# A hybrid recurrent step on one core: two chunks in one triangular matrix, and a 128-row contraction for the samples' updates

## The chip, the cores and the metric

The kernel runs on one core of a Trainium2 chip. The metric is the device time of one execution in microseconds (us). The core has TensorE (PE in the profile, with its weight loads as PEld), VectorE (DVE), ScalarE (ACT), GpSimd (POOL) and a queue engine, SyncE (SP), which here issues nearly all DMAs. Each engine works through its own instructions in order; semaphores tie them together.

## The reference

One layer of a decoder with three token mixers fed by one projection, then a gated feed-forward part. There is one prompt of 512 tokens and a batch of 8 samples of 4 tokens each. The mixers are a gated delta rule, an mLSTM and HGRN2, with 4 heads of 128 channels each. The delta rule is what the change touches most. Cut to that:

```
G = cumsum(g);  decay = exp(G[t] - G[s]) for s <= t
A = tril(beta[t] * decay * (k k^T), -1)
rhs = beta * (v - exp(G) * (k S))
u = solve (I + A) u = rhs                  # unit lower triangular
o = exp(G) * (q S) + (tril(q k^T) * decay) u
S' = exp(G[last]) * S + (k * exp(G[last] - G))^T u
```

All three mixers end a chunk with a state update of the last form, `S' = decay * S + K^T U`. For the samples that is one update for each of 8 samples and 4 heads.

## The kernel before

**Big matrix products.** The dense products (`gemm`, `step`) run as three fp32r matmuls for each 128x128 weight tile and half of the tokens: high part by high part, high by low, low by high. Each has 272 moving columns. In the trace they are `mm_..` tiles, written 128x272. There are 165 such products, and they fill TensorE from the start to the end.

**Background work.** The mixers are Python generators that `spawn` puts beside the dense products and `drive`/`stage` advance a piece at a time, so the pieces stand between the matmuls of the dense products. A counter of estimated TensorE time (`tick`) sets the spacing: after each `yield` a generator stays away for some 3.2 of it. A scheduler of the framework then fixes the order of each engine at build time. TensorE thus executes the mixers' small matmuls (fp32, tiles `bank_..`) in a fixed place among the wide ones. If the input of one is not there, all of TensorE waits.

**The delta rule of a prompt head** (`gdn`, u = 0 to 3) works on four chunks of 128 tokens. The inverse of each unit triangular matrix is made by doubling. `small_inverse` first inverts the 16x16 blocks on the diagonal: it sends the matrix out to DRAM and back with blocks as rows, does 15 pairs of small operations on VectorE, and goes out and back again. Then POOL spreads the blocks over a block-diagonal 128x128 matrix, in both orientations X and Y, four chunks wide (`gen_g__2779` and `gen_g__2782` for head 0). Three levels of doubling follow, for blocks of 16, 32 and 64. A level is, for each of four chunks:

```
pp[c] = Nn[c]^T Y[c];  Pn = mask(pp)
z[c]  = X[c]^T Pn[c];  Y += z
z[c]  = Pn[c]^T X[c];  X += z        # not at the last level
```

Nn is the triangular matrix with its axes exchanged by a TensorE transpose (`to_tok`). That makes 12, 12 and 8 fp32 matmuls of 128x128 and 4 transposes a head. Then a chain over the chunks uses Y[c] to get u (`zb`) and the next state.

**The samples' updates** (`state_update`, once for each of 8 samples in `mlstm`, `gdn` and `hgrn`, u = 4). `stack` splits K and U into high and low parts, sends them to DRAM (`ku`), rearranges them (`k`) and loads them into the tile `kuv`. There 48 rows hold data (three products of parts, 4 heads, 4 tokens), and rows 32 to 63 were zeroed at the start, so rows 48 to 63 stay zero. `uexp` on POOL spreads U over the four heads with a mask; one fp32r matmul, contracting over the 64 rows of `kuv`, gives the update of all four heads (64x512 in the trace). For the mLSTM a second, tiny one with `nm` (64x4) updates the normaliser. A group `32x128` ahead of it (`inter`) multiplies the queries into the state, in four column groups of 32.

**Other lines that the steps touch.** `masks` loads the 0/1 masks `cu` in stretches of 512 columns through the two `y` buffers and casts them on POOL. Line 118 is the matmul helper, line 123 the transpose, line 92 the two-input elementwise helper, lines 697 to 704 the DMAs of `stack`.

Of the kernel before, what the change touches and what calls it, by code (L numbers as in the profile page):

```python
# [9 lines left out]
F32 = mybir.dt.float32  # L10
F32R = mybir.dt.float32r
# [33 lines left out]
K_BM = 640  # L45
K_HM, K_NM = K_BM, K_BM + 4
K_SG = K_BM + 8
K_BD = K_SG + 1
N_CF = K_BD + 128

U_X1, U_Y1, U_HL = 0, 128, 256
U_LV = U_HL + 7 * 64
N_CU = U_LV + 4 * 128


class Build:
# [348 lines left out]
    def gate_rows(self, ps, sign, bi, ea, rst, RB, R1, R2, rp):  # L405
        self.lab = "_ga_"
        self.act(self.identr, self.ident)
        self.act(self.nm, self.cf[:64, K_NM:K_NM + H])
# [4 lines left out]
        Z, SP, GF, T, i2, l2, m = (row() for _ in range(7))  # L413
# [18 lines left out]
        I3, i2, l2, m = (t[G3] for t in (T, i2, l2, m))  # L432
# [53 lines left out]
        c = self.cst  # L486
# [4 lines left out]
        for k, R in ((1, R2), (0, R1)):  # L491
            self.lab = "_ga_"
            b = self.bank()
# [3 lines left out]
            b = self.bank()  # L497
# [332 lines left out]

    def small_inverse(self, Nt, out):

        lab = self.lab
        z = self.dr.tile([8 * 8208], F32, tag="nt", name="nt")
        self.qs.dma_start(out=z[0:65536].rearrange("(p x) -> p x", p=128), in_=Nt.rearrange("p c t -> p (c t)"))
        yield 4
        zb = z.rearrange("(b x) -> b x", b=8)[:, 0:8192].rearrange("b (j c t) -> b j c t", j=16, c=4)
        DT = self.gen()[:32]
        D = DT[:, 0:256].rearrange("p (j i) -> p j i", j=16)
        for c in range(4):  # L840
            self.qs.dma_start(out=D[8 * c:8 * c + 8], in_=zb[:, :, c, 0:16])
# [23 lines left out]
        mk = self.cf[:, K_BD:K_BD + 128].rearrange("p (b j) -> p b j", b=8).unsqueeze(1).to_broadcast([128, 4, 8, 16])  # L865
        for x in range(2):
            t = self.slots(4)
            z = Z[:, 4 * x:4 * x + 4, :].unsqueeze(2).to_broadcast([128, 4, 8, 16])
            self.mul(t.rearrange("p c (b j) -> p c b j", b=8), z, mk, self.g)
            out.append(t)  # L870


    def gdn(self, q, k, vv, u):
        lab = "_g%d_" % u
        self.lab = lab
        prompt = u < H
        n = 4 if prompt else 1
# [48 lines left out]
        if not prompt:  # L926
            mb = lambda o: bn(self.cu[:, o:o + 128])
# [8 lines left out]
        b = self.to_tok(vv)  # L936
# [1 line left out]
        self.mul(nv, b, self.bc(nk, 128))  # L938
        yield
        if prompt:  # L940
            while len(XY) < 2:
                yield 2
            X, Y = XY
            yield self.WSP
        lv = (16, 32, 64) if prompt else (2,)
        for m in lv:
            self.lab = lab
            i = STEPS.index(m)
            pp = self.sbank(n)
            for c in range(n):  # L950
                self.mm(pp[:, c, :], Nn[:, c, :], Y[:, c, :])
            Pn = self.slots(n)
            self.mul(Pn, pp, bn(self.cu[:, U_LV + 128 * i:U_LV + 128 * i + 128]))
            yield
            self.lab = lab
            z = self.sbank(n)
            for c in range(n):
                self.mm(z[:, c, :], X[:, c, :], Pn[:, c, :])
            self.add(Y, Y, z)
            if m != lv[-1]:  # L960
                z = self.sbank(n)
                for c in range(n):
                    self.mm(z[:, c, :], Pn[:, c, :], X[:, c, :])
                self.add(X, X, z)
            yield
        self.lab = lab
        if prompt:
            S = None
# [30 lines left out]
            o = self.sbank(4)  # L999
# [4 lines left out]
        else:  # L1004
# [27 lines left out]
            o = self.sbank(1)  # L1032
# [466 lines left out]
    def run(self):  # L1499
        with self.pool("cst") as self.cst, self.pool("wp") as self.wp, self.pool("hp", 8) as self.hp, \  # L1500
# [15 lines left out]
            with self.pool("gp", self.NG1) as self.gp:  # L1516
                with self.tc.tile_pool(name="dr", bufs=2, space=bass.MemoryType.DRAM) as self.dr, self.pool("smp") as self.smp, self.pool("stp", 4) as self.stp, \
# [48 lines left out]
def _consts():  # L1566
    s = np.arange(128)[:, None]
    t = np.arange(128)[None, :]
    cf = np.zeros((128, N_CF), np.float32)
# [7 lines left out]
    def level(m):  # L1577
        return (s // (2 * m) == t // (2 * m)) & (s % (2 * m) < m) & (t % (2 * m) >= m)
# [109 lines left out]
```

## Time and profile before

| | us |
|---|---|
| median of 3 runs | 1167.66 (1166.32 to 1168.19) |
| the profiled execution | 1167.82 |
| its span, first to last instruction | 1165.8 |
| TensorE busy | 1148.9 (99%) |
| VectorE busy | 730.6 (63%) |
| ScalarE busy | 454.1 (39%) |
| GpSimd busy | 195.7 (17%) |
| mean granted TensorE clock | 0.994 of full |

How to read it: matmuls are pipelined, so what one costs the engine is the distance from its start to the start of the next one, not its own duration. A wide matmul shows 0.29 us of its own and the next starts 0.126 us later. A fp32 matmul of 128x128 has two records, so "x8" is four matmuls. The time that an instruction waits stands in brackets behind it, with what ended the wait.

### The profile page before, as it was taken

What the parts mean: (1) busy time and instruction counts of PE and PEld (TensorE: products, weight loads), DVE (VectorE), ACT (ScalarE), POOL (GpSimd) and SP (SyncE); (2) the same over time, 40 slices, a digit from 0 to 9 for tenths busy, and PEclk for the clock granted to TensorE, in tenths of its full rate; (3) what the DMA queues carried; (4) which work ended last, traced back from release to release, by engine and by line L of the source; (5) the groups of instructions that cost most, each with busy time, mean ns of one, the idle gap of its engine ahead of it and who ended that gap; (6) DMA issues with size and microseconds to landing.
All of it is one profiled execution on the core that took longest, in us unless ns stands there. A gap on an engine that the chain in (4) does not pass through costs nothing.

```text
span 1165.8 us, 23742 instructions
## 1 busy us (share of the span) xinstructions
PE 1148.9 (99%) x9249; PEld 1126.0 (97%) x9249; DVE 730.6 (63%) x1762; ACT 454.1 (39%) x890; POOL 195.7 (17%) x662
## 2 busy tenths in 40 slices
PE   8999999999999999999999999999999999999996
PEld 8999989999999999899979999999999999999996
DVE  6876588767758666687545265476765336767532
ACT  6653454525326322332323334444443224444431
POOL 3000040101010212211142001112221002222112
PEclk9999999999999999999989999999999999999998
DMA  7232343221322334411544253222222232222332
GB/s 240 73 97 84 111 124 119 70 78 55 80 81 76 116 101 140 132 55 58 144 120 131 82 169 92 89 77 88 91 92 82 76 101 88 91 91 80 91 98 77
DMA packets 51956, 114.84 MB, mean 99 GB/s; under 512 B 11557, under 2 KB 19493, under 8 KB 51749
## 3 DMA queue, kind: packets, MB, share of 16 engines
q1 hardware_dynamic: 51124, 112.41, 31.4%
q8 instruction: 73, 1.20, 0.4%
q10 hardware_dynamic: 720, 0.92, 0.2%
q14 instruction: 39, 0.31, 0.1%
HBM read 100.92 MB, written 13.57 MB: 98 GB/s over the span
## 4 chain that ended last, share of the span: by engine, by line
PE 94%; DMA 3%; issue 1%; DVE 1%; POOL 1%; SPq 0%; ACT 0%; POOLq 0%; DVEq 0%; ACTq 0%
DMA k<-ku 1%; DMA kuv<-k 1%; PE mm_fl__14120 L118 1%; PE mm_ff__11778 L118 1%; PE mm_ff__11610 L118 1%; PE mm_ff__11442 L118 1%; PE mm_ff__13664 L118 1%; PE mm_ff__14016 L118 1%; PE mm_ff__13840 L118 1%; PE mm_ff__13576 L118 1%; PE mm_ff__11274 L118 1%; PE mm_ff__13928 L118 1%; PE mm_ff__13752 L118 1%; PE mm_ff__11358 L118 1%; PE mm_ff__11862 L118 1%
## 5 line engine op out<-in xcount | busy, mean ns | idle before, releaser
L113 ACT ACTIVATE whi<-raw 128x512 fp32r<-128x512 f32 x320 | 199.6, 625 | 495.7 <-DMA raw<-in_wdn 10.2
L92 DVE TENSOR_TENSOR wlo<-raw,whi 128x512 fp32r<-128x512 f32 x320 | 220.6, 690 | 178.4 <-ACT whi L113 169.6
L110 DVE SCALAR_TENSOR_TENSOR y<-U,cols,y 128x560 f32<-128x560 f32 (+1 forms) x124 | 100.9, 815 | 21.2 <-ACT y L113 19.5
L113 ACT ACTIVATE y<-U,cols 128x560 f32<-128x560 f32 (+1 forms) x56 | 46.8, 838 | 23.5 <-DVE U L92 23.0
L1361 POOL COPY fso<-U 128x2 f32<-128x2 f32 x44 | 28.9, 656 | 79.3 <-DVE U L92 79.3
L1358 POOL COPY U<-fst 128x16 f32<-128x16 f32 x44 | 27.0, 617 | 81.3 <-DVE y L110 40.7
L113 ACT ACTIVATE sg<-y 128x560 f32<-128x560 f32 (+1 forms) x34 | 22.9, 674 | 18.6 <-DVE y L110 18.5
L110 DVE SCALAR_TENSOR_TENSOR col<-col,col 128x4 f32<-128x4 f32 (+2 forms) x146 | 24.4, 168 | 7.6 <-ACT junk L113 4.6
L113 ACT ACT_TABLE_LOAD x16 | 20.5, 1283 | 2.7 <-DVE gen_de__2292 L110 0.9
L92 DVE TENSOR_TENSOR col<-col 128x4 f32<-128x4 f32 (+2 forms) x73 | 12.8, 175 | 1.5
L92 POOL TENSOR_TENSOR tot<-tot 128x32 f32<-128x32 f32 (+5 forms) x25 | 8.2, 329 | 13.2 <-DVE gen_ph__5506 L92 9.5
L107 DVE TENSOR_SCALAR col<-col 128x4 int32<-128x4 int32 (+4 forms) x32 | 5.6, 175 | 5.3 <-ACT junk L113 4.8
L135 POOL MEMSET gen_ff__12370<- 1x1 f32 x1 | 0.1, 88 | 51.9 <-PE mm_ff__11862 L118 51.9
L1362 POOL COPY fso<-U 128x16 f32<-128x16 f32 x44 | 8.5, 194 | 0.0
L135 POOL MEMSET gen_bh__8978<- 1x1 f32 x1 | 0.1, 89 | 46.6 <-DVE gen_bh__8730 L92 46.6
L110 DVE SCALAR_TENSOR_TENSOR hlo<-xn,cols,hhi 128x544 fp32r<-128x544 f32 x8 | 6.3, 785 | 1.8 <-ACT hhi L113 1.8
L113 ACT ACTIVATE hhi<-xn,cols 128x544 fp32r<-128x544 f32 x8 | 6.0, 751 | 1.5 <-DVE xn L92 1.5
L607 POOL COPY gso<-U 128x3 f32<-128x3 f32 x12 | 3.2, 266 | 20.3 <-ACT U L113 20.3
L105 DVE TENSOR_SCALAR col<-col 128x4 int32<-128x4 int32 (+4 forms) x38 | 6.2, 162 | 0.6
L604 POOL COPY U<-gst 128x24 f32<-128x24 f32 x12 | 3.8, 318 | 14.8 <-DVE gen_g__2447 L92 5.0
L110 DVE SCALAR_TENSOR_TENSOR xin<-xin,rp,gen_nr__469 128x544 f32<-128x544 f32 x8 | 5.6, 780 | 0.0
L92 DVE TENSOR_TENSOR hlo<-xin,hhi 128x544 fp32r<-128x544 f32 x8 | 5.2, 717 | 0.0
(5021 smaller groups left out, 4804.4 us busy)
## 6 DMA issues: line engine op xcount, KB each, us to landing
raw<-in_wp SPq DMA_DIRECT2D x47, 512.0 KB, 3.8
raw<-in_wup SPq DMA_DIRECT2D x44, 512.0 KB, 3.5
raw<-in_wgt SPq DMA_DIRECT2D x24, 512.0 KB, 3.4
raw<-in_wdn SPq DMA_DIRECT2D x16, 512.0 KB, 4.0
raw<-in_wbr SPq DMA_DIRECT2D x24, 256.0 KB, 2.7
raw<-in_wout SPq DMA_DIRECT2D x8, 512.0 KB, 3.4
raw<-in_wdn SPq DMA_DIRECT2D x16, 192.0 KB, 2.4
xin<-in_xt SPq DMA_DIRECT2D x8, 272.0 KB, 6.6
```

Source lines behind the costliest of these rows:

```text
L92: (eng or self.v).tensor_tensor(out=out, in0=a, in1=b, op=op)
L105: (eng or self.v).tensor_scalar(out=out, in0=a, scalar1=s1, scalar2=None, op0=op0)
L107: (eng or self.v).tensor_scalar(out=out, in0=a, scalar1=s1, scalar2=s2, op0=op0, op1=op1)
L110: self.v.scalar_tensor_tensor(out=out, in0=a, scalar=sc, in1=b, op0=op0, op1=op1)
L113: self.s.activation(out=out, in_=a, func=func, **kw)
L118: self.pe.matmul(out, lhsT=lhsT, rhs=rhs, start=start, stop=stop)
L135: self.g.memset(x[(slice(0, 1),) * len(x.shape)], 0.0)
L604: self.g.tensor_copy(out=sv[:, :, 0:3], in_=self.gst[:, tile_i, :, :])
L607: self.g.tensor_copy(out=self.gso[:, tile_i, 0, :], in_=U[:, 512:515])
L1358: self.g.tensor_copy(out=sv[:, :, 0:2], in_=self.fst[:, i, :, :])
L1361: self.g.tensor_copy(out=self.fso[:, i, 0, :], in_=U[:, 512:514])
L1362: self.g.tensor_copy(out=self.fso[:, i, 1:9, :], in_=sv[:, :, 4:6])
```

## The change

For the prompt heads, chunks 0 and 1 share one matrix, and chunks 2 and 3 another. The even chunk's triangle lies below the diagonal (it is transposed by TensorE), the odd chunk's above it as it was; `NP` holds their sum. `small_inverse` gives one matrix W for two chunks, with the block masks now applied by VectorE from the 8-bit masks. A level of doubling is now, for each of two pairs: a transpose of W, a product of NP with the masked W, one masking operation for both (VP), one product z, one addition into W, and one masking of W for the next level. After the last level W is transposed once more, and Y of the even and odd chunks is cut out of W and of its transpose.

For the samples, `kuv`, `nm` and the mask of `uexp` have 128 rows; rows 64 to 127 are zeroed at the start, and the matmuls contract over all 128. The sample part of `gdn` computes what it did; its code is written out. The masks `cu` grow from 1216 to 1856 columns, and `cf` loses 128.

```diff
 def uexp(self, b):
-        t = self.gen(dt=F32R)[:64].rearrange("p (h e) -> p h e", h=4)
-        self.mul(t, self.ku[:, b, 128:256].unsqueeze(1).to_broadcast([64, 4, 128]),
-                 self.bc(self.cf[:64, K_HM:K_HM + 4], 128), self.g)
+        t = self.gen(dt=F32R).rearrange("p (h e) -> p h e", h=4)
+        self.mul(t, self.ku[:, b, 128:256].unsqueeze(1).to_broadcast([128, 4, 128]),
+                 self.bc(self.cf[:, K_HM:K_HM + 4], 128), self.g)
 def small_inverse(self, Nt, out):
         self.act(XY[:, 1], X.rearrange("p i j -> p j i"))
+        self.sub(X, X, self.eye, self.g)
 ...
-        mk = self.cf[:, K_BD:K_BD + 128]...to_broadcast([128, 4, 8, 16])
-        for x in range(2):
-            t = self.slots(4)
-            z = Z[:, 4 * x:4 * x + 4, :].unsqueeze(2).to_broadcast([128, 4, 8, 16])
-            self.mul(t.rearrange("p c (b j) -> p c b j", b=8), z, mk, self.g)
-            out.append(t)
+        z = Z[:, 1:4:2, :]
+        self.add(z, z, Z[:, 4:8:2, :], self.g)
+        mk = self.cu[:, U_BD:U_BD + 128]...to_broadcast([128, 2, 8, 16])
+        t = self.slots(4)
+        self.mul(t[:, 0:2, :].rearrange("p c (b j) -> p c b j", b=8), z.unsqueeze(2).to_broadcast([128, 2, 8, 16]), mk)
+        out.append(t)
 def gdn(self, q, k, vv, u):
-        bt = self.to_tok(Nt)
-        Nn = self.slots(n)
-        self.act(Nn, bt)
+        if prompt:
+            bt = self.to_tok(Nt[:, 0::2, :])
+            NP = self.slots(2)
+            self.add(NP, bt, Nt[:, 1::2, :])
 ...
-            X, Y = XY
-        for m in lv:
-            pp = self.sbank(n)
-            for c in range(n):
-                self.mm(pp[:, c, :], Nn[:, c, :], Y[:, c, :])
-            Pn = self.slots(n)
-            self.mul(Pn, pp, bn(self.cu[:, U_LV + 128 * i:U_LV + 128 * i + 128]))
-            yield
-            z = self.sbank(n)
-            for c in range(n):
-                self.mm(z[:, c, :], X[:, c, :], Pn[:, c, :])
-            self.add(Y, Y, z)
-            if m != lv[-1]:
-                z = self.sbank(n)
-                for c in range(n):
-                    self.mm(z[:, c, :], Pn[:, c, :], X[:, c, :])
-                self.add(X, X, z)
-            yield
+            W, Wm = XY[0][:, 0:2, :], XY[0][:, 2:4, :]
+            self.mul(Wm, W, mb(U_PR))
+            for i in range(len(STEPS)):
+                pp = self.sbank(4)
+                for c in range(2):
+                    self.tr(pp[:, c, :], W[:, c, :])
+                for c in range(2):
+                    self.mm(pp[:, 2 + c, :], NP[:, c, :], Wm[:, c, :])
+                VP = self.slots(4)
+                self.mul(f4(VP), f4(pp), mk.unsqueeze(2).to_broadcast([128, 2, 2, 128]))
+                yield
+                z = self.sbank(2)
+                for c in range(2):
+                    self.mm(z[:, c, :], VP[:, c, :], VP[:, 2 + c, :])
+                self.add(W, W, z)
+                if i + 1 < len(STEPS):
+                    self.mul(Wm, W, mb(U_PR + 256 * i + 256))
+                yield
+            b = self.to_tok(W)
+            Y = self.slots(4)
+            self.mul(Y[:, 0::2, :], W, mb(U_UP))
+            self.mul(Y[:, 1::2, :], b, mb(U_UP))
 def run(self):
-                    self.ku = mc.tile([64, NB, 256], F32R, name="kuv")
-                    self.nm = mc.tile([64, H], F32R, name="nm")
+                    self.ku = mc.tile([128, NB, 256], F32R, name="kuv")
+                    self.nm = mc.tile([128, H], F32R, name="nm")
                     self.g.memset(self.ku[32:64].bitcast(F32), 0.0)
+                    self.g.memset(self.ku[64:128].bitcast(F32), 0.0)
```

Two places in the order of the instructions. The first is TensorE at head 0's first level of doubling. Before, `bank_g__2980` is pp, `gen_g__2782` is Y, `gen_g__2779` X, and 3000 and 3006 belong to head 1:

```order
L118 MATMUL bank_g__2980<-gen_g__2782,gen_g__2506 128x128 x4
L118 MATMUL bank_g__3000<-gen_pg__2618,gen_pg__2746 128x128 x4
L123 MATMUL bank_g__3006<-cf,gen_pg__2618 128x128 x4
...
L118 MATMUL bank_g__3029<-gen_g__2985,gen_g__2779 128x128 x4
L118 MATMUL bank_g__3035<-gen_g__2779,gen_g__2985 128x128 x4
```

Now `gen_g__2789` holds W and masked W, `bank_g__2994` takes the transposes and the product, and `bank_g__3056` is z (3008 belongs to head 1):

```order
L125 MATMUL bank_g__2994<-cf,gen_g__2789 128x128 x2
L120 MATMUL bank_g__3008<-gen_pg__2621,gen_pg__2749 128x128
L120 MATMUL bank_g__2994<-gen_g__2789,gen_g__2508 128x128 x2
...
L120 MATMUL bank_g__3056<-gen_g__2999 128x128 x2
```

Twelve matmuls of the head became four and two transposes; the place among the wide matmuls is nearly the same. In all, `bank_g` has 238 fp32 matmuls of 128x128 before and 158 now, and 85 transposes before and 109 now.

The second place is on TensorE at the samples of HGRN2. `bank_h__7471` transposes K, which starts the way of the data through `stack`; `bank_h__7710` is the first matmul that reads `kuv`. Before, 120 wide matmuls lie between the two:

```order
L123 MATMUL bank_h__7471<-cf,smp 128x128
...
L123 MATMUL bank_h__7542<-cf,gen_h__7436 128x128 x4
L118 MATMUL bank_h__7554<-sl_h__7264,sl_h__7259 128x128
...
L118 MATMUL bank_h__7554<-gen_h__7667,xp 32x128 x4
...
L118 MATMUL bank_h__7710<-gen_h__7664,kuv 128x512
```

Now the transpose is `bank_h__7544` and the first reader of `kuv` is `bank_h__7735`:

```order
L125 MATMUL bank_h__7544<-cf,smp 128x128
...
L125 MATMUL bank_h__7560<-cf,gen_h__7488 128x128 x4
L120 MATMUL bank_h__7591<-sl_h__7305,sl_h__7300 128x128
...
L120 MATMUL bank_h__7591<-gen_h__7679,xp 32x128 x4
...
L120 MATMUL bank_h__7735<-gen_h__7676,kuv 128x512
```

There are 99 wide matmuls between them now, and seven fp32 matmuls and four transposes of heads 2 and 3 that stood between them before now stand ahead of the transpose. On the SP queue, which carries the data out and back, this stood there before:

```order
L697 DMA ku<-gen_h__7557 128x512
L698 DMA ku<-gen_h__7559 128x256
L718 DMA gen_h__7816<-in_hS 128x512
L701 DMA k_7588<-ku 4x8x3072
L718 DMA gen_h__7873<-in_hS 128x512
L718 DMA gen_h__7933<-in_hS 128x512
L163 DMA raw<-in_wgt 128x1024
L704 DMA kuv<-k_7588 16x8x256 x3
```

And now:

```order
L699 DMA ku<-gen_h__7594 128x512
L700 DMA ku<-gen_h__7596 128x256
L720 DMA gen_h__7945<-in_hS 128x512
L703 DMA k_7625<-ku 4x8x3072
L165 DMA raw<-in_wgt 128x1024
L706 DMA kuv<-k_7625 16x8x256 x2
L720 DMA gen_h__8005<-in_hS 128x512
L706 DMA kuv<-k_7625 16x8x256
```

Two loads of a sample's state that stood ahead of the loads of `kuv` are issued earlier, and one now stands ahead of the third of them.

## Rows read from the trace of the kernel before

**Rows 1.** The page, part 1: busy time and share of the span.

```profile
PE 1148.9 (99%) x9249; PEld 1126.0 (97%) x9249; DVE 730.6 (63%) x1762; ACT 454.1 (39%) x890; POOL 195.7 (17%) x662
```

**Rows 2.** Chain of waits: start us, length us, what; a dense product of 48.

```profile
635.44 6.05 PE mm_bh__8247 L118 x48
```

**Rows 3.** TensorE's timeline at a doubling: start us, us, engine line op out<-in xcount.

```profile
226.91 1.06 PE L118 MATMUL bank_g__3000<-gen_pg__2618,gen_pg__2746 128*128 128x128 f32 x8
227.80 0.60 PE L123 MATMUL bank_g__3006<-cf,gen_pg__2618 128*128 128x128 f32 x4
228.16 0.37 PE L118 MATMUL mm_bm__3318<-hhi,wlo 128*128 128x272 f32 x1
```

**Rows 4.** TensorE's timeline around two samples' updates.

```profile
456.43 0.50 PE L118 MATMUL bank_g__6079<-gen_g__5958,kuv 64*128 64x512 f32 x1
456.86 0.39 PE L118 MATMUL mm_ph__6012<-hhi,whi 128*128 128x272 f32 x1
457.08 0.29 PE L118 MATMUL mm_ph__6012<-hlo,whi 128*128 128x272 f32 x1
...
488.52 0.28 PE L118 MATMUL mm_ph__6503<-hlo,whi 128*128 128x272 f32 x1
488.74 0.50 PE L118 MATMUL bank_g__6455<-gen_g__6359,kuv 64*128 64x512 f32 x1
489.16 0.40 PE L118 MATMUL mm_ph__6503<-hhi,wlo 128*128 128x272 f32 x1
489.40 0.28 PE L118 MATMUL mm_ph__6503<-hhi,whi 128*128 128x272 f32 x1
```

**Rows 5.** TensorE's timeline: a matmul of the same width over 128 rows.

```profile
190.53 0.40 PE L118 MATMUL bank_g__2588<-rl,identr 128*128 128x512 f32 x1
190.76 0.29 PE L118 MATMUL mm_pg__2632<-hlo,whi 128*128 128x272 f32 x1
```

**Rows 6.** TensorE's timeline at HGRN2's samples; in brackets the wait ahead and its end.

```profile
567.12 0.27 PE L123 MATMUL bank_h__7471<-cf,smp 128*128 128x128 f32 x1
...
585.43 0.29 PE L118 MATMUL mm_bg__7645<-hhi,wlo 128*128 128x272 f32 x1
588.13 0.79 PE L118 MATMUL bank_h__7710<-gen_h__7664,kuv 64*128 64x512 f32 x1 [2.40 <-POOL gen_h__7664 L92]
...
589.24 0.43 PE L118 MATMUL mm_bg__7725<-gen_bg__6901,whi 128*128 128x272 f32 x1
589.47 0.43 PE L118 MATMUL mm_bg__7725<-gen_bg__6899,wlo 128*128 128x272 f32 x1
```

**Rows 7.** Windows: busy us of each engine, then granted clock, DMA share, GB/s.

```profile
580.00:600.00 20.00, 17.59 (x112) 15.87 (x112) 7.72 (x15) 3.56 (x6) 10.66 (x16) 0.83 0.47 109
```

**Rows 8.** The SP queue's timeline at the same place.

```profile
572.44 0.59 SPq L701 DMA_DIRECT2D k<-ku  x1
...
578.99 1.28 SPq L704 DMA_DIRECT2D kuv<-k  x3
```

**Rows 9.** POOL's timeline: the first spreading of U, HGRN2's, then the delta rule's.

```profile
586.93 1.15 POOL L92 TENSOR_TENSOR gen_h__7664<-kuv,cf 64x512 fp32r<-64x512 f32 x1 [12.98 <-DMA kuv<-k]
...
450.91 1.15 POOL L92 TENSOR_TENSOR gen_g__5958<-kuv,cf 64x512 fp32r<-64x512 f32 x1 [11.06 <-DMA kuv<-k]
```

**Rows 10.** TensorE's timeline: the matmul whose result the delta rule's samples send out.

```profile
435.00 0.38 PE L118 MATMUL bank_g__5816<-r,sl_g__5046 128*128 128x128 f32 x2
```

**Rows 11.** POOL's timeline: head 0's blocks are spread.

```profile
222.90 1.09 POOL L92 TENSOR_TENSOR gen_g__2779<-gen_g__2719,cf 128x512 f32<-128x512 f32 x1 [2.82 <-DMA gen_g__2719<-xy]
223.95 1.54 POOL L92 TENSOR_TENSOR gen_g__2782<-gen_g__2719,cf 128x512 f32<-128x512 f32 x1
```

**Rows 12.** VectorE's timeline: the masking of pp at two levels.

```profile
229.58 0.67 DVE L92 TENSOR_TENSOR gen_g__2985<-bank_g__2980,cu 128x512 f32<-128x512 f32 x1
...
256.22 0.69 DVE L92 TENSOR_TENSOR gen_g__3407<-bank_g__3402,cu 128x512 f32<-128x512 f32 x1 [0.87 <-PE bank_g__3402 L118]
```

**Rows 13.** Groups by line and shape: count, busy us, mean ns of one, idle before.

```profile
L92 DVE TENSOR_TENSOR gen_ph__5231<-gen_ph__5231,tot 128x256 f32<-128x256 f32 x6 | 2.6, 438 | 3.1 <-PE bank_h__5932 L118 1.1 <-PE bank_h__5870 L118 1.1 <-PE bank_h__5726 L118 0.9
```

More of the change, by code (lines that the diff above doesn't have):

```diff
@@ L32 @@
 LEVELS = (1, 2, 4, 8, 16, 32, 64)
-STEPS = (2, 16, 32, 64)
+STEPS = (16, 32, 64)
 C_LNFFN, C_LNFIN = 0, 8
@@ L47 @@
 K_SG = K_BM + 8
-K_BD = K_SG + 1
-N_CF = K_BD + 128
+N_CF = K_SG + 1
 U_X1, U_Y1, U_HL = 0, 128, 256
 U_LV = U_HL + 7 * 64
-N_CU = U_LV + 4 * 128
+U_PR = U_LV + 128
+U_UP = U_PR + 3 * 256
+U_BD = U_UP + 128
+N_CU = U_BD + 128
 class Build:
@@ L407, in gate_rows @@
         self.act(self.identr, self.ident)
-        self.act(self.nm, self.cf[:64, K_NM:K_NM + H])
+        self.act(self.nm, self.cf[:, K_NM:K_NM + H])
         G0, G1, G2, G3 = (slice(32 * i, 32 * i + 4) for i in range(4))
@@ L864, in small_inverse @@
         self.lab = lab
-        mk = self.cf[:, K_BD:K_BD + 128].rearrange("p (b j) -> p b j", b=8).unsqueeze(1).to_broadcast([128, 4, 8, 16])
-        for x in range(2):
-            t = self.slots(4)
-            z = Z[:, 4 * x:4 * x + 4, :].unsqueeze(2).to_broadcast([128, 4, 8, 16])
-            self.mul(t.rearrange("p c (b j) -> p c b j", b=8), z, mk, self.g)
-            out.append(t)
+        z = Z[:, 1:4:2, :]
+        self.add(z, z, Z[:, 4:8:2, :], self.g)
+        mk = self.cu[:, U_BD:U_BD + 128].rearrange("p (b j) -> p b j", b=8).unsqueeze(1).to_broadcast([128, 2, 8, 16])
+        t = self.slots(4)
+        self.mul(t[:, 0:2, :].rearrange("p c (b j) -> p c b j", b=8), z.unsqueeze(2).to_broadcast([128, 2, 8, 16]), mk)
+        out.append(t)
     def gdn(self, q, k, vv, u):
@@ L922, in gdn @@
         self.lab = lab
-        bt = self.to_tok(Nt)
-        Nn = self.slots(n)
-        self.act(Nn, bt)
-        if not prompt:
-            mb = lambda o: bn(self.cu[:, o:o + 128])
+        mb = lambda o: self.cu[:, o:o + 128].unsqueeze(1).to_broadcast([128, n // 2 or 1, 128])
+        if prompt:
+            bt = self.to_tok(Nt[:, 0::2, :])
+            NP = self.slots(2)
+            self.add(NP, bt, Nt[:, 1::2, :])
+        else:
+            bt = self.to_tok(Nt)
+            Nn = self.slots(n)
+            self.act(Nn, bt)
             self.v.copy_predicated(Y, mb(U_Y1), Nt)
@@ L940, in gdn @@
         if prompt:
-            while len(XY) < 2:
+            while not XY:
                 yield 2
-            X, Y = XY
+            W, Wm = XY[0][:, 0:2, :], XY[0][:, 2:4, :]
             yield self.WSP
-        lv = (16, 32, 64) if prompt else (2,)
-        for m in lv:
             self.lab = lab
-            i = STEPS.index(m)
-            pp = self.sbank(n)
-            for c in range(n):
-                self.mm(pp[:, c, :], Nn[:, c, :], Y[:, c, :])
-            Pn = self.slots(n)
-            self.mul(Pn, pp, bn(self.cu[:, U_LV + 128 * i:U_LV + 128 * i + 128]))
+            self.mul(Wm, W, mb(U_PR))
@@ new lines, in gdn @@
+            for i in range(len(STEPS)):
[5 more added lines that the diff above has]
+                VP = self.slots(4)
+                mk = self.cu[:, U_PR + 256 * i:U_PR + 256 * i + 256].rearrange("p (k t) -> p k t", k=2)
+                f4 = lambda t: t.rearrange("p (k c) t -> p k c t", k=2)
+                self.mul(f4(VP), f4(pp), mk.unsqueeze(2).to_broadcast([128, 2, 2, 128]))
+                yield
+                self.lab = lab
+                z = self.sbank(2)
[5 more added lines that the diff above has]
+                yield
+                self.lab = lab
@@ L954, in gdn @@
+            b = self.to_tok(W)
+            Y = self.slots(4)
+            self.mul(Y[:, 0::2, :], W, mb(U_UP))
+            self.mul(Y[:, 1::2, :], b, mb(U_UP))
+        else:
+            self.lab = lab
+            pp = self.sbank(1)
+            self.mm(pp[:, 0, :], Nn[:, 0, :], Y[:, 0, :])
+            Pn = self.slots(1)
+            self.mul(Pn, pp, mb(U_LV))
             yield
             self.lab = lab
-            z = self.sbank(n)
-            for c in range(n):
-                self.mm(z[:, c, :], X[:, c, :], Pn[:, c, :])
+            z = self.sbank(1)
+            self.mm(z[:, 0, :], X[:, 0, :], Pn[:, 0, :])
@@ L959, in gdn @@
             self.add(Y, Y, z)
-            if m != lv[-1]:
-                z = self.sbank(n)
-                for c in range(n):
-                    self.mm(z[:, c, :], Pn[:, c, :], X[:, c, :])
-                self.add(X, X, z)
-            yield
+        yield
         self.lab = lab
@@ L1582, in _consts @@
     cf[:, K_NM:K_NM + H] = hm & (s // 16 != 1)
-    cf[:, K_BD:K_BD + 128] = s // 16 == t // 16
     cf[:, K_SG] = 1.0
@@ L1588, in _consts @@
     cu[:, U_Y1:U_Y1 + 128] = level(1)
+    cu[:, U_LV:U_LV + 128] = level(2)
     for i, m in enumerate(STEPS):
-        cu[:, U_LV + 128 * i:U_LV + 128 * (i + 1)] = level(m)
+        second = (s % (2 * m)) >= m
+        cu[:, U_PR + 256 * i:U_PR + 256 * i + 128] = (s // m == t // m) & np.where(second, s <= t, s >= t)
+        cu[:, U_PR + 256 * i + 128:U_PR + 256 * i + 256] = level(m) | level(m).T
+    cu[:, U_UP:U_UP + 128] = s <= t
+    cu[:, U_BD:U_BD + 128] = s // 16 == t // 16
     cu[:, U_X1:U_X1 + 128] = level(1).T
```

## The prediction

> **What bounds the kernel now.** I read the busy shares first. TensorE is busy for 1148.9 us of a span of 1165.8 [rows 1], so all its waits, the head and the tail of the kernel together are 16.9 us. VectorE has 63%, the others less. So the time is the sum of what TensorE's instructions cost at their places in its order, and a change counts in two ways: by the issue time that it takes out of TensorE, and by new waits ahead of a small matmul whose input is late, behind which every wide one stands too.
>
> The second view gives the unit. A dense product of 48 wide matmuls takes 6.05 us in the chain of waits [rows 2], so one costs 6.05 / 48 = 0.126 us. Third, the timeline of TensorE at a doubling, read from start to start [rows 3]: four fp32 matmuls of 128x128 from 226.91 to 227.80, 0.89 us or 0.223 each; four transposes from 227.80 to 228.16, 0.36 us. Behind a group of transposes the next wide matmul takes 0.37 instead of 0.29, so I add 0.08: 0.44 for four, 0.11 each.
>
> **Part 1, the doubling: -15.2 us.** Before, a head has 12 + 12 + 8 = 32 fp32 matmuls and 4 transposes: 32 x 0.223 + 4 x 0.11 = 7.58 us. Now a level has 2 transposes, 2 products and 2 z; the head adds 2 transposes for NP and 2 for the last W: 12 x 0.223 + 10 x 0.11 = 3.78 us. That is 3.80 a head and 15.2 for four. The order confirms the counts (80 fp32 matmuls fewer, 24 transposes more: 17.84 - 2.64 = 15.2). All of it is issue time on the engine that sets the end, so all of it counts, if no wait takes its place.
>
> What could wait: each level still goes to VectorE and back twice. The masking of pp (128x512) takes 0.67 to 0.69 us; once it began at 229.58, over 1.5 us after the last matmul of its level could have ended, once directly behind it, after 0.87 us of waiting for TensorE [rows 12]. So VectorE answers in 0.7 to some 2.5 us, and in the order of both kernels wide matmuls worth about 3 us or more stand between the two halves of a level. The way from z back to the product is now an addition and a masking of 256 columns in place of an addition of 512: two at 0.438 [rows 13] for one at 0.69, 0.2 us more plus a hand-over inside VectorE. It fits under those 3 us. I price it at nothing; without that cover each of 24 hand-overs would cost what it is late.
>
> VectorE's own load: maskings 3 x 0.69, additions 3 x 0.44, maskings of W 3 x 0.44, two cuts of Y, one NP and one spreading at 0.44 each, about 6.4 us a head against 8 x 0.69 = 5.5 before. At 63% that moves nothing. ScalarE loses a copy. Of the longer masks the first are needed only well after their loads; nothing.
>
> **Part 2, the first level of a head: +0.5 us (0 to +2).** POOL's two spreadings, 1.09 and 1.54 us, go [rows 11]. In their place stand a small POOL addition, one VectorE spreading and one masking (0.44 each), with two hand-overs between engines; nearest to 2.6 us, so about equal. But head 0 had only some 0.5 us in hand: POOL ended at 223.95 + 1.54 = 225.5 and TensorE came to this place shortly before 226.9. If VectorE is at another long operation when the blocks land, that is 0.7 or twice that, for one or two of four heads.
>
> **Part 3, 128 rows: -6.5 us (0 to -7.5).** What a 64-row update costs now, from start to start [rows 4]: one that stands alone among wide matmuls makes the wide one ahead 0.22 (488.52 to 488.74), takes 0.42 itself, and the one behind takes 0.24: 0.88 for three. A matmul of the same width over 128 rows starts at 190.53 and the wide one behind it at 190.76: 0.23 [rows 5]. So three would be 0.126 + 0.23 + 0.126 = 0.48, and 0.40 are saved. One that stands directly behind the `inter` group shows 0.43 and then 0.22 (456.43, 456.86, 457.08); there the way back from the 32-column tiles has to be paid all the same, which I put at 0.22 - 0.126 = 0.10: 0.65 now, 0.23 + 0.10 + 0.126 = 0.46 then, 0.19 saved. By the order 16 of the 24 updates stand behind such a group, 8 alone: 16 x 0.19 + 8 x 0.40 = 6.2. The 8 normaliser matmuls mostly stand next to an update; 0.3 together, up to 1.2 if three more stand alone. Nothing would be saved if the time lay in the matmul's width and not in the change between shapes; the 0.23 in [rows 5] is nearest, the same width and type, so I take 6.5.
>
> Here a rule speaks against the change. The Trainium skill, "TensorE: Matmul & The Clock Gate", section "Why this matters for your kernels", says that a single matmul over 32 rows takes the same time as one over 128, and that the gain of fewer rows lies in running several at once. By it part 3 would be 0 and the kernel some 1156 us; the rows above, 0.42 with 0.10 on either side against 0.23, do not agree.
>
> POOL spreads U over 128 partitions instead of 64: the free size, which sets its 1.15 us [rows 9], is the same. Zeroing 64 more rows lies at the start, before anything reads them.
>
> **Part 4, the samples of HGRN2: +3.0 us (0.7 to 4.6).** This is the one place where TensorE waits long [rows 6]. The transpose at 567.12 sends K on its way; POOL waits 12.98 us for `kuv`, starts at 586.93 and takes 1.15 [rows 9]; the first update starts at 588.13, 21.0 us after the transpose. TensorE was free at 585.43 + 0.13 = 585.56, so 18.4 after the transpose, and stood 2.6 us. Now, between the same two points, 21 wide matmuls, seven fp32 matmuls and four transposes are missing: 21 x 0.126 + 7 x 0.223 + 0.44 = 4.6, so TensorE is there after 13.8 us. If the chain keeps its 21.0 the wait is 7.2. The same chain for the delta rule's samples took 452.06 - 435.00 = 17.1 [rows 9, 10]; with 17.1 the wait is 3.3. The SP queue issued `k` at 572.44 and `kuv` at 578.99 [rows 8]; two state loads that stood ahead of them are now issued earlier, which speaks for the shorter chain, and one now stands ahead of the third load of `kuv`, which speaks for the longer. Against 2.6 that is +0.7 to +4.6; I take +3.
>
> After this wait the wide matmuls cost 0.23 instead of 0.126 (589.24 to 589.47), and the granted clock of the window is 0.83 [rows 7]: TensorE ran at the lower level, 1.2 GHz, for some 24 of them, 24 x 0.1 = 2.5 us. I take this as staying as it is, since the clock fell after a wait of 2.6 and will fall after a longer one too.
>
> The samples of the delta rule have 21.4 us from 435.00 to 456.43 for a chain of 17.1, and about the same after; 0.
>
> **The sum.** 1167.8 (the profiled execution; the median is 0.16 lower, so it is a usual one) - 15.2 + 0.5 - 6.5 + 3.0 = 1149.6, say 1149.5.
>
> **The rivals.**
> (B) The 128 rows save nothing, because the time lies in the width: 1149.5 + 6.5 = 1156. For it: only one row shows the 128-row price, and it stands beside other 128-row work of its own kind. Against it: the 64-row one also lengthens its neighbours. Chance 0.10.
> (C) The waits grow: the chain of HGRN2 keeps 21.0 or more and two or three heads wait 1 us at their first level: +1.6 + 3 = 1154.5. For it: TensorE arrives everywhere sooner while the DMA chains keep their length. Chance 0.12.
> (D) The chain of HGRN2 falls to some 15 us because the queue ahead of it is empty: a wait of 1.2 in place of the 5.6 of the forecast, and the clock holds behind it: 1149.5 - 4.4 - 2.5 = 1142.6. For it: fewer loads ahead on SP. Against it: the delta rule's chain, also with little ahead, took 17.1. Chance 0.05.
> (E) Slower than before: VectorE answers the hand-overs of the doubling later than TensorE needs them. There are 24 (two a level, three levels, four heads), and the gain is 18.3 us, so it decides from 18.3 / 24 = 0.76 us each; at 1.0 the time is 1149.5 + 24 = 1173.5. For it: VectorE is often behind its queue (the 229.58 of [rows 12]), and the way from z has one step more. Against it: some 3 us of wide matmuls cover each. Chance 0.03.
> That the change does not do what it says is excluded by the order's counts.
>
> **How the numbers follow.** The forecast has 0.70, with 1146.5 to 1152.5 for its own bounds. The range goes down to 1144, half way and more to (D), and up to 1157, which takes in (B) and (C); outside lie (D), (E) and sums of (B) with (C). A measurement of this kernel can tell about 0.2%, 2.3 us, from no change. All cases but (E) lie more than that below 1167.7: faster 0.96, and of the rest 0.01 same, 0.03 slower.
>
> **What would show it.** Part 1: in the costliest groups, fp32 matmuls of `bank_g` reduced by 80 and no bracketed wait ahead of the pp and z groups of a head; a wait of about 1 us there in most levels means (E). Part 2: a wait ahead of head 0's first level in place of none. Part 3: updates written 128*128 with 0.23 (alone) or 0.33 with the way back (behind `inter`) to the next start; 0.42 means (B). Part 4: the bracket ahead of the first 128x512 update of HGRN2 between 3.3 and 7.2 us, and wide matmuls at 0.23 behind it; a bracket near nothing and 0.126 means (D). The forecast is wrong if TensorE's idle time in the span rises by more than 8 us over 16.9, or if its issue time falls by less than 15.

## The result, and the profile after

The changed kernel takes 1149.47 us (median of 4 runs, 1148.69 to 1150.29) against 1167.47 (1166.32 to 1168.19): 0.9847 of before, 95% interval 0.983 to 0.9864, 18.0 us less. 1149.5 was forecast.

Part 1 of the page, busy time and share of the span, answers to [rows 1]:

```profile
PE 1130.4 (99%) x9113; PEld 1111.8 (97%) x9113; DVE 729.9 (64%) x1782; ACT 451.9 (39%) x886; POOL 190.7 (17%) x664
```

The span is 1147.2. TensorE's busy time fell by 18.5, its idle time stayed: 1147.2 - 1130.4 = 16.8 against 16.9. In the idle time the wait at HGRN2's samples grew by 1.8 us; the waits at the start of the kernel (`mm_fi` in the view of waits) happen to be 1.2 us shorter in this execution, 2.6 against 3.8. VectorE's load did not move (730.6 before).

The waits of TensorE (line, what it waited for, us in total, times, longest):

```profile
PE bank_h__7735 L120 <- POOL gen_h__7676 L94: 4.2, 1, 4.2
...
PE bank_g__6019 L120 <- POOL gen_g__5898 L94: 0.2, 1, 0.2
```

The first is the wait of HGRN2's samples, 2.4 before [rows 6]. No matmul of a doubling is in the list. The last one is the delta rule's first update, which did not wait before (456.43 in [rows 4]).

Head 0's first level on TensorE, then on VectorE, answers to [rows 3, 12]:

```profile
226.15 0.44 PE L125 MATMUL bank_g__2994<-cf,gen_g__2789 128*128 128x128 f32 x2
226.42 0.39 PE L120 MATMUL bank_g__3008<-gen_pg__2621,gen_pg__2749 128*128 128x128 f32 x2
226.64 0.68 PE L120 MATMUL bank_g__2994<-gen_g__2789,gen_g__2508 128*128 128x128 f32 x4
...
230.40 0.61 PE L120 MATMUL bank_g__3056<-gen_g__2999 128*128 128x128 f32 x4
230.85 0.38 PE L125 MATMUL bank_g__3073<-cf,gen_g__2934 128*128 128x128 f32 x2
```

```profile
226.12 0.43 DVE L94 TENSOR_TENSOR gen_g__2789<-gen_g__2789,cu 128x256 f32<-128x256 f32 x1
228.09 0.68 DVE L94 TENSOR_TENSOR gen_g__2999<-bank_g__2994,cu 128x512 f32<-128x512 f32 x1
```

Two products take 0.45 from start to start (230.40 to 230.85), 0.225 each, as before. The masked W is there at 226.12 + 0.43 = 226.55, 0.09 us ahead of the product that reads it. The transposes ahead need only W, so they cover the masking. VP, the second row of VectorE, is there at 228.09 + 0.68 = 228.77, z starts at 230.40: 1.6 us of cover are left.

An update that stands alone, one behind an `inter` group, and one behind an `inter` group with the tiny normaliser matmul behind it, on TensorE; these answer to [rows 4]:

```profile
475.54 0.29 PE L120 MATMUL mm_ph__6453<-hhi,wlo 128*128 128x272 f32 x1
475.67 0.40 PE L120 MATMUL bank_g__6471<-gen_g__6369,kuv 128*128 128x512 f32 x1
475.90 0.28 PE L120 MATMUL mm_ph__6453<-hhi,whi 128*128 128x272 f32 x1
476.03 0.29 PE L120 MATMUL mm_ph__6453<-hlo,whi 128*128 128x272 f32 x1
```

```profile
444.09 0.50 PE L120 MATMUL bank_g__6092<-gen_g__6016,kuv 128*128 128x512 f32 x1
444.43 0.29 PE L120 MATMUL mm_ph__6074<-hhi,whi 128*128 128x272 f32 x1
444.55 0.29 PE L120 MATMUL mm_ph__6074<-hlo,whi 128*128 128x272 f32 x1
```

```profile
156.16 0.43 PE L120 MATMUL bank_m__1932<-gen_m__2093,xp 128*32 128x129 f32 x8
156.52 0.50 PE L120 MATMUL bank_m__2154<-gen_m__2100,kuv 128*128 128x512 f32 x1
156.86 0.17 PE L120 MATMUL bank_m__2160<-nm,kuv 128*128 128x4 f32 x1
156.89 0.37 PE L120 MATMUL mm_pg__2190<-hhi,whi 128*128 128x272 f32 x1
157.10 0.29 PE L120 MATMUL mm_pg__2190<-hlo,whi 128*128 128x272 f32 x1
```

Alone: 0.13, 0.23, 0.13 in place of 0.22, 0.42, 0.24. Behind `inter`: 0.34, and 0.12 for the wide one behind it, in place of 0.43 and 0.22. With the normaliser behind it: 0.34, 0.03, then 0.21 for the wide one, so some of what is saved comes back on the next matmul.

HGRN2's samples on TensorE, POOL and the SP queue, answer to [rows 6, 8, 9]; in brackets the wait and what ended it:

```profile
560.43 0.27 PE L125 MATMUL bank_h__7544<-cf,smp 128*128 128x128 f32 x1
...
574.08 0.29 PE L120 MATMUL mm_bg__7706<-hhi,wlo 128*128 128x272 f32 x1
578.53 0.80 PE L120 MATMUL bank_h__7735<-gen_h__7676,kuv 128*128 128x512 f32 x1 [4.16 <-POOL gen_h__7676 L94]
579.12 0.43 PE L120 MATMUL mm_bg__7706<-hhi,whi 128*128 128x272 f32 x1
579.35 0.43 PE L120 MATMUL mm_bg__7706<-hlo,whi 128*128 128x272 f32 x1
```

```profile
577.43 1.04 POOL L94 TENSOR_TENSOR gen_h__7676<-kuv,cf 128x512 fp32r<-128x512 f32 x1 [9.34 <-DMA kuv<-k]
```

```profile
564.32 0.59 SPq L703 DMA_DIRECT2D k<-ku  x1
...
571.11 0.80 SPq L706 DMA_DIRECT2D kuv<-k  x2
```

TensorE is free at 574.2, 13.8 us after the transpose, to the tenth what was forecast. The chain took 578.53 - 560.43 = 18.1 us. Behind the wait the wide matmuls cost 0.23. The window of that stretch (columns as in [rows 7]) has a granted clock of 0.50, the lower level, 1.2 GHz:

```profile
578.50:584.40 5.90, 5.87 (x25) 5.78 (x26) 2.65 (x5) 0.63 (x1) 5.90 (x6) 0.50 0.35 98
```

### The profile page after: what moved, and what is told of

It is laid out like the page before. It is cut to its first block, busy times and chain, and to the rows that moved or that the text cites. A ratio compares the mean times of both kernels' runs of the same rounds, so it can differ in the third digit from the quotient of the medians.

```text
span 1147.2 us, 23487 instructions
## 1 busy us (share of the span) xinstructions
PE 1130.4 (99%) x9113; PEld 1111.8 (97%) x9113; DVE 729.9 (64%) x1782; ACT 451.9 (39%) x886; POOL 190.7 (17%) x664
## 4 chain that ended last, share of the span: by engine, by line
PE 93%; DMA 3%; issue 1%; POOL 1%; SPq 1%; ACT 0%; DVE 0%; POOLq 0%; DVEq 0%; ACTq 0%
DMA kuv<-k 1%; DMA k<-ku 1%; PE mm_fl__14080 L120 1%; PE mm_ff__11738 L120 1%; PE mm_ff__11570 L120 1%; PE mm_ff__11402 L120 1%; PE mm_ff__13624 L120 1%; PE mm_ff__13976 L120 1%; PE mm_ff__13800 L120 1%; PE mm_ff__13536 L120 1%; PE mm_ff__11234 L120 1%; PE mm_ff__13888 L120 1%; PE mm_ff__13712 L120 1%; PE mm_ff__11822 L120 1%; PE mm_ff__11654 L120 1%
## 5 line engine op out<-in xcount | busy, mean ns | idle before, releaser
L112 DVE SCALAR_TENSOR_TENSOR y<-U,cols,y 128x560 f32<-128x560 f32 (+1 forms) x124 | 100.8, 814 | 20.9 <-ACT y L115 18.9
L112 DVE SCALAR_TENSOR_TENSOR col<-col,col 128x4 f32<-128x4 f32 (+2 forms) x146 | 26.9, 189 | 7.2 <-ACT junk L115 4.5
L115 ACT ACTIVATE sg<-y 128x560 f32<-128x560 f32 (+1 forms) x34 | 22.9, 675 | 20.3 <-DVE y L112 20.2
L606 POOL COPY U<-gst 128x24 f32<-128x24 f32 x12 | 4.4, 366 | 18.2 <-DVE y L112 11.2
L275 POOL CAST cu<-y 128x512 uint8<-128x512 f32 (+1 forms) x4 | 5.4, 1358 | 3.2 <-DMA y<-in_cu 3.2
L120 PE MATMUL mm_bg__7706<-hhi,whi 128*128 128x272 f32 x16 | 5.8, 366 | 0.0
```

Of the source, the lines that this page charges most:

```text
L112: self.v.scalar_tensor_tensor(out=out, in0=a, scalar=sc, in1=b, op0=op0, op1=op1)
L115: self.s.activation(out=out, in_=a, func=func, **kw)
L120: self.pe.matmul(out, lhsT=lhsT, rhs=rhs, start=start, stop=stop)
L275: self.g.tensor_copy(out=self.cu[:, c0:c0 + n], in_=t)
L606: self.g.tensor_copy(out=sv[:, :, 0:3], in_=self.gst[:, tile_i, :, :])
```

## The experiments

The first four were made to part the three terms of the sum: the doubling, the 128 rows, the wait. e1 undoes the samples' part of the change:

```diff
-        t = self.gen(dt=F32R).rearrange("p (h e) -> p h e", h=4)
+        t = self.gen(dt=F32R)[:64].rearrange("p (h e) -> p h e", h=4)
...
-                    self.ku = mc.tile([128, NB, 256], F32R, name="kuv")
-                    self.nm = mc.tile([128, H], F32R, name="nm")
+                    self.ku = mc.tile([64, NB, 256], F32R, name="kuv")
+                    self.nm = mc.tile([64, H], F32R, name="nm")
```

> The changed kernel with the samples' updates back at 64 rows, so the doubling is the only part left. The prediction's terms: 1149.5 + 6.5 = 1156. The updates' rows in the trace of the changed kernel, added up one by one, give less, 5 us: 1154.5. Rival (the 128 rows save nothing and the doubling brought all 18 us): 1149.5. In all cases the wait at HGRN2's samples stays near 4.2 us, since the order around it is that of the changed kernel.

Measured: 1157.0 (1156.87 to 1158.28), 0.992 of before (0.9906 to 0.9933); before had 1166.44 on that chip. Only 9.4 us for the doubling, where 14.7 less some 3 for the wait was forecast. The trace shows a second wait, at the delta rule's first update, and the windows (busy us of each engine, granted clock, DMA share, GB/s) the clock behind it:

```profile
442.50 0.50 PE L120 MATMUL bank_g__6018<-gen_g__5897,kuv 64*128 64x512 f32 x1 [1.46 <-POOL gen_g__5897 L94]
```

```profile
440.00:450.00 10.00, 8.54 (x61) 7.28 (x60) 5.55 (x13) 1.77 (x3) 4.65 (x11) 0.83 0.24 75
```

e2 is the kernel before with that part alone (the same lines, the other way).

> The kernel before with only the samples' updates at 128 rows. The prediction's term: 1167.5 - 6.5 = 1161. By the rows added up one by one: 1162.5. Rival (a 64-row matmul costs by its width, nothing saved): 1167.5. An update alone among wide matmuls should show 0.13, 0.23, 0.13 from start to start instead of 0.22, 0.42, 0.24; the wait at HGRN2's samples stays at 2.4.

Measured: 1160.52 (1159.11 to 1161.58), 0.9949 (0.9936 to 0.9961): 5.9 us for the updates. In its profiled execution the wait at HGRN2 is there and the clock did not fall: the granted clock from 580 to 600 us is 1.00, and the wide matmuls behind the wait start 0.12 apart:

```profile
583.92 0.50 PE L118 MATMUL bank_h__7711<-gen_h__7665,kuv 128*128 128x512 f32 x1 [2.32 <-POOL gen_h__7665 L92]
584.26 0.29 PE L118 MATMUL mm_bg__7726<-gen_bg__6900,whi 128*128 128x272 f32 x1
584.38 0.28 PE L118 MATMUL mm_bg__7726<-gen_bg__6902,whi 128*128 128x272 f32 x1
```

e3 lets HGRN2's samples stay away longer between the loads of `kuv` and its first reader; nothing else changes.

```diff
         for p in range(3):
             self.sy.dma_start(out=self.ku[16 * p:16 * p + 16].bitcast(F32), ...)
-        yield self.WDM
+        yield 12 if lab.startswith('_h') else self.WDM
```

> The changed kernel with the first reader of kuv in HGRN2 put later, so that 150 wide matmuls instead of 99 lie between the transpose and it: 20.1 us by their prices against a chain of 18.1. If the wait (4.2) and the lower clock behind it (24 matmuls at 0.10 more, 2.4) both go and nothing takes their place: 1149.5 - 6.6 = 1143. Rival 1 (the clock there falls without the wait too): 1145.3. Rival 2 (the wait turns up at the next instruction that needs a chain, or the tail grows by what is moved): 1149.5.

Measured: 1143.89 (1143.28 to 1147.1), 0.9812 (0.9798 to 0.9826). Wait and lower clock both went (granted clock 1.00 from 570 to 590 us), and nothing took their place at HGRN2. But the delta rule's first update now waited, though the edit does not touch its place in TensorE's order; the clock did not fall behind this wait (1.00 from 436 to 450 us):

```profile
439.99 0.51 PE L120 MATMUL bank_g__6019<-gen_g__5898,kuv 128*128 128x512 f32 x1 [1.12 <-POOL gen_g__5898 L94]
```

e4 is the same edit in the kernel before (8 in place of 12).

> The kernel before with the same edit, 144 wide matmuls instead of 120 between the two, 21.4 us by their prices against a chain of 21.0. If the wait (2.4 to 2.6) and the lower clock (2.5) go: 1167.5 - 5 = 1162.5. Rival 1: 1165. Rival 2: 1167.5. Against e3 this gives the change's effect without the wait: if the forecast's terms for the doubling and the updates hold, e3 lies 15.2 - 0.5 + 6.5 = 21 under it; by the rows of the changed kernel, some 20.

Measured: 1162.99 (1162.67 to 1163.24), 0.9969 (0.9957 to 0.998), no wait at a sample's update of HGRN2. So that wait and its clock cost the kernel before 3.5 us in the median of its runs; the 5 expected are what the one profiled execution of before shows.

From here on the waits of these two places could be taken out of both kernels, so that the terms stand nearly alone. One wait is left that differs: the mLSTM's first update waited 1.1 to 1.2 us in the traces of e4, e6 and e7, but 0.3 in that of e5. e5 is e3 with 10 for the delta rule as well:

```diff
-        yield self.WDM
+        yield {'g': 10, 'h': 12}.get(lab[1], self.WDM)
```

> The changed kernel with the first reader of kuv put later for HGRN2 as in e3 and for the delta rule too (150 wide matmuls instead of 126 between r's product and it). In e3 the delta rule's samples still waited 1.1 us, in e1 1.5 with the lower clock behind it. If those waits go and nothing takes their place: e3's 1143.9 - 1.1 = 1142.8, down to 1141.5 where the clock fell behind the wait in some runs. Rival (the later work ends later somewhere else): 1144 or more.

Measured: 1142.14 (1141.3 to 1142.62), 0.9787 (0.9774 to 0.9801): the fastest of all, 6 to 7 us under the changed kernel. TensorE is busy without a gap in both places and its clock is full; the windows:

```profile
430.00:450.00 20.00, 20.00 (x171) 19.21 (x171) 12.88 (x32) 4.80 (x9) 6.36 (x14) 1.00 0.48 134
570.00:590.00 20.00, 20.00 (x171) 18.87 (x169) 8.37 (x16) 4.78 (x8) 11.60 (x14) 1.00 0.47 129
```

e6 is e5 with 64-row updates (e1's edit), e7 is e4 with 128-row ones.

> e5 with 64-row updates: the doubling alone, without the two waits. Against e4 (before, 1163.0, no wait at HGRN2): by the prediction's term -15.2 + 0.5, 1148.3; if the waits and not the doubling made e1 poor, it must come out there; if the doubling itself brings only the 9.4 us that e1 showed, 1153.6. e5 lies under it by the updates' share: 6.5 by the forecast, 5.5 by the rows added up, 0 by the rival.

> e4 with 128-row updates: the updates alone, without the wait at HGRN2. By the prediction's term 1163.0 - 6.5 = 1156.5; by the rows added up 1157.5; by the rival that the 128 rows save nothing 1163. In e2 the wait of 2.3 was there but the granted clock did not fall behind it in the profiled execution; here there is no wait, so that cannot blur the share.

Measured: e6 1148.45 (1148.15 to 1149.56), 0.9846 (0.9832 to 0.9859); e7 1157.17 (1156.85 to 1157.23), 0.9916 (0.9903 to 0.993). So the doubling brings 1162.99 - 1148.45 = 14.5; the updates bring 1162.99 - 1157.17 = 5.8 in the kernel before and 1148.45 - 1142.14 = 6.3 in the changed one, of which the mLSTM's wait may be some 0.9. The rival that one of them saves nothing is out. e1 was 8.5 above e6: about what two waits (4.1 and 1.5 in its trace) and two stretches at the lower clock cost there.

e8 asks why a 64-row update is dear. It issues each of them twice in the kernel before; it also puts HGRN2's first reader of `kuv` later than e4 does, 18 in place of 8.

```diff
-        yield self.WDM
+        yield 18 if lab.startswith('_h') else self.WDM
...
         self.mm(kv, kw, ux.rearrange("p h e -> p (h e)"))
+        self.mm(kv, kw, ux.rearrange("p h e -> p (h e)"))
```

> The kernel before with each of the 24 updates issued twice in a row at 64 rows, the second one writing the same result again. If the time of a 64-row update lies in the change between shapes, the first starts 0.23 us ahead of the second, as the 128-row one does with its own kind behind it, and the second takes the 0.42: 24 x 0.23 = 5.5 us more on TensorE. If it lies in the 64-row matmul itself, both take 0.42: 10 us more. The places shift a little with it, so the rows decide, not the total.

Measured: 1175.79 in one run, 9.3 above before. The total also has a wait of 3.6 us at HGRN2's first update: in this order only 114 wide matmuls stand ahead of it, in spite of the 18. TensorE's busy time, which leaves waits out, is 1155.3 against 1148.9: 6.4 more, nearer to the 5.5 than to the 10. The rows are clearer. The same update as in the first lines of [rows 4], on TensorE:

```profile
460.17 0.73 PE L118 MATMUL bank_g__6087<-gen_g__5966,kuv 64*128 64x512 f32 x2
460.83 0.39 PE L118 MATMUL mm_ph__6020<-hhi,whi 128*128 128x272 f32 x1
461.06 0.29 PE L118 MATMUL mm_ph__6020<-hlo,whi 128*128 128x272 f32 x1
```

The pair takes 0.66 where one took 0.43 (456.43 to 456.86), and the wide one behind it 0.23 as before. A second 64-row update among its own kind costs 0.23, what a 128-row one costs: the rest is the change of shape. By these rows and [rows 4] it costs 0.2 us in the first matmul and 0.1 on either neighbour. The Trainium skill, "TensorEngine Tiling (Array Packing)", section "Key Properties", says that a change of the tiling mode drains the engine. These rows agree with it, though none shows the drain itself.

e9 asks why the delta rule's chain had become longer. In the changed kernel a 512 KB load of weights stands between the two `ku` transfers on the SP queue, before it did not. On top of e3's edit, one copy of U is made on VectorE behind the subtraction and so is ready later, and the two transfers come to stand together:

```diff
             for i in hs:
-                self.act(at(i), (K, U)[x])
+                if i != 5:
+                    self.act(at(i), (K, U)[x])
             self.sub(at(lo), (K, U)[x], at(hs[0]))
+            if x:
+                self.v.tensor_copy(out=at(5), in_=U)
```

> e3 with one copy of U (the second part) made on VectorE behind the subtraction instead of on ScalarE, so that the two ku transfers of the delta rule's samples stand next to each other on the SP queue, behind the 512 KB load of weights that stood between them. If that load between them is what made the chain of the delta rule's samples 21.5 us long (17.1 before), k is issued some 2.6 us after the second ku instead of 4.4 and the chain falls to 18 to 19.5: the wait of 1.1 at the delta rule's first update goes, 1142.5 to 1143. Rival (the load takes its share of the transfer time wherever it stands, and the load between the kuv transfers counts as much): the chain stays at 21 to 22, the wait at about 1, time 1143.9 as e3.

Measured: 1143.05 (1142.69 to 1144.71), 0.9795 (0.9782 to 0.9809), with before at 1167.52. The ratio does not tell it from e3; the trace does. The SP queue:

```profile
419.60 0.33 SPq L165 DMA_DIRECT2D raw<-in_wp  x1
420.02 0.38 SPq L702 DMA_DIRECT2D ku<-gen_g__5743  x1
420.45 0.42 SPq L703 DMA_DIRECT2D ku<-gen_g__5745  x1
425.04 0.62 SPq L706 DMA_DIRECT2D k<-ku  x1
431.64 0.81 SPq L709 DMA_DIRECT2D kuv<-k  x2
432.55 0.36 SPq L165 DMA_DIRECT2D raw<-in_wp  x1
432.96 0.43 SPq L709 DMA_DIRECT2D kuv<-k  x1
```

`k` is issued 4.6 us after the second `ku` (4.4 in the changed kernel, 2.6 before), and the wait is still 1.1. That the load stands between the two is not the cause; my theory falls. In the kernel before the load ahead of `ku` was issued 1.8 us earlier and none stood among the loads of `kuv`. The other traces speak for the rival on record, that the load counts wherever it stands. HGRN2's samples in e8, a kernel without the new doubling, have a 512 KB load 0.4 us ahead of the first `ku`, and there too `k` comes 4.6 us after the second, though a 256 KB load follows 1.9 us behind the second as well. In all traces and for all three mixers it is 4.4 to 4.6 us with such a load within half a microsecond of the `ku` transfers, and 1.8 to 3.0 without. No run moves that load alone. It would be some 1.8 of the 4.5 us by which the chain grew; another 1.9 lie between the first load of `kuv` and POOL, and no run explains those.

e10 halves the wait: e3 with 6 in place of 12.

> The changed kernel with 114 wide matmuls instead of 99 ahead of HGRN2's first update: the wait falls from 4.2 to 2.3. Behind a wait of 2.4 (before) the granted clock fell in the profiled execution, behind one of 2.3 (e2) it did not, behind 4.2 (changed) it did. If it falls as often as behind 4.2, the time is 1149.5 - 1.9 = 1147.6; if it does not fall, 1145.1, and the mean granted clock of the run is 0.996 instead of 0.994.

Measured: 1148.53 (1147.21 to 1150.01), 0.9841 (0.9827 to 0.9854), mean granted clock 0.993 or 0.994 in all five runs. The wait is shorter than the 2.3 expected, 1.75, and the clock falls behind it nevertheless, here four matmuls later. The delta rule's first update waits 1.1 here, as in e3:

```profile
578.79 0.51 PE L120 MATMUL bank_h__7753<-gen_h__7707,kuv 128*128 128x512 f32 x1 [1.75 <-POOL gen_h__7707 L94]
579.14 0.28 PE L120 MATMUL mm_bg__7700<-hhi,whi 128*128 128x272 f32 x1
...
579.51 0.43 PE L120 MATMUL mm_bg__7700<-hhi,whi 128*128 128x272 f32 x1
```

## Why the prediction was right, and where it was not

| term | forecast | measured |
|---|---|---|
| doubling and first level of a head | -15.2 + 0.5 = -14.7 | -14.5 (e6 under e4) |
| 128 rows | -6.5 | -5.8 (e7 under e4), -6.3 (e5 under e6) |
| samples' waits and their clock | +3.0 | +2.8 |
| sum | -18.2 | -18.0 |

The last term is the difference of two: the changed kernel lies 6.3 over e5 (1149.47 less the 1.0 by which before was slower in that set, less 1142.14), before 3.5 over e4. The rows are the steps of one path, before, e4, e6, e5, changed, so with the 6.3 they give -18.0 whatever their sizes; what tests the forecast is each row for itself, and e7 for the updates. The interval of a ratio is about 0.0013 to either side, 1.5 us, so the agreement to a few tenths is partly luck.

**Doubling: right.** Counting matmuls and transposes and pricing them from start to start gave the term; no wait took its place, so (E), 24 late hand-overs, is out, and with it the waits of the heads in (C), whose sum comes to 1154.1, not the 1154.5 of the prediction. The forecast's cover was right too (1.6 us left at head 0's first level).

**First level: the cause was off.** I had priced 0.5 us for VectorE being late. It was not; at head 0 the order puts the transposes of W and one matmul of head 1 ahead of the product, and that covers the masking with 0.09 us to spare, and no other head's first level is in the list of waits. So the doubling proper was forecast at 15.2 and measured at 14.5. Added up from start to start, with what the wide matmul behind each group takes over 0.126, the 128x128 matmuls and transposes of `bank_g` cost 63.8 us in the trace of before and 48.8 in that of the changed kernel, 15.0 less; between e4 and e6 it is 14.8.

**128 rows: right, by the row that was taken.** The 0.23 of [rows 5] is what the updates cost. The terms are 0.40 alone and 0.19 behind `inter`, as forecast; the mLSTM's updates behind `inter` with the normaliser behind them gave 0.09 instead (0.34, 0.10, 0.23 before, at 156.43 of its trace; 0.34, 0.03, 0.21 now), since the wide matmul behind a matmul of 4 columns still takes 0.21. That is a part of what is missing to 6.5. (B) is out.

**HGRN2's wait: right in kind, the size lucky.** The chain took 18.1, between the two bounds of 17.1 and 21.0; the wait of 4.2 lies in the 3.3 to 7.2 forecast, but +1.8 and not +3. The chain became 1.4 us shorter at the start (the way from the transpose to `k` took 3.9 instead of 5.3) and 1.6 at the end (from the first `kuv` to POOL 6.3 instead of 7.9); why, no run shows. (D), a chain of 15, is out.

**The step that failed: "The samples of the delta rule have 21.4 us from 435.00 to 456.43 for a chain of 17.1, and about the same after; 0."** The time was the same, the chain was not. From the matmul whose result is sent out to the first update, on TensorE and POOL, where [rows 4, 9, 10] show 17.1 and 21.4:

```profile
417.47 0.38 PE L120 MATMUL bank_g__5738<-r,sl_g__5013 128*128 128x128 f32 x2
...
439.17 0.50 PE L120 MATMUL bank_g__6019<-gen_g__5898,kuv 128*128 128x512 f32 x1 [0.18 <-POOL gen_g__5898 L94]
```

```profile
438.07 1.04 POOL L94 TENSOR_TENSOR gen_g__5898<-kuv,cf 128x512 fp32r<-128x512 f32 x1 [13.17 <-DMA kuv<-k]
```

It ends at 439.11, 21.6 us after its start: 4.5 longer than before. 4.3 us of slack were used up, and the rest is a wait of 0.2 in this execution, 1.1 in e3 and 1.5 with the lower clock in e1; without it e5 is 1.75 under e3, little more than the interval. It is no accident of one execution: the chain took 17.1 to 17.4 us in the traces of all five kernels with the old doubling (e2, the 128 rows alone, 17.1) and 21.6 to 23.5 in all seven with the new one (e1, the doubling alone, 22.9). So the term put at nothing had lost its slack with the new order. I had looked for what moves on TensorE, not at what stands around these transfers on the SP queue.

**The clock: "staying as it is" was too simple.** The mean clock of the kernel before lies between 0.992 and 0.996 from execution to execution, mostly the shorter the higher, and in e2 the clock did not fall behind a wait of 2.32. That the stretch at 1.2 GHz is not there every time fits this, and would explain why e4 brought 3.5 and not 5; it is not shown, since e4, without that wait, also varies from 0.994 to 0.997. The changed kernel, with the longer wait, shows 0.993 to 0.995. A part of the +2.8, which I had put on the wait alone, may be this.

## What to carry to other kernels

On an engine that is busy 99% of the span, count instructions and price them from start to start, neighbours included: that gave 21.7 us for the doubling and the updates where 20.9 were measured (e5 under e4). Here a matmul over 64 rows among full ones paid for the change of shape on both sides, and padding its contraction with zero rows was cheaper. When an engine gets faster, look at every chain of transfers that it used to cover, and at what the new order puts beside the transfers: here one wait grew, another chain became longer and used up its slack, and moving the readers later, one line, gave another 6 to 7 us.

## What the runs showed of the hardware that was not expected

The granted clock fell to 1.2 GHz behind waits of TensorE of 4.16 (changed), 2.40 (before), 1.75 (e10) and 1.46 us (e1), and not behind waits of 1.12 (e3) and 2.32 (e2). Within this case the length of the wait alone does not decide. In the changed kernel the stretch lasts from 578.5 to 584.3, 24 wide matmuls at about 0.1 more, 2.4 us on top of the wait of 4.16.

The chain of the delta rule's samples, with the same transfers and bytes, took between 17.1 and 23.5 us in these kernels (the last in e5, 418.07 to 441.55). The part from the second `ku` to `k` is longer where a load of weights is issued within half a microsecond of the `ku` transfers; what lengthens the rest stays open.
